# Attention's q and k as seven-product units in the first projection, with q, k and v kept in DRAM until they are used

## The chip, the cores and the metric

The kernel runs on one core of one Trainium2 chip. The metric is the device time of one execution in microseconds, from runs on the chip; a profile of one more execution shows what each engine did. TensorE (PE) multiplies into the eight banks of PSUM; VectorE (DVE), ScalarE (ACT) and GpSimd (POOL) compute; SyncE (SP) and POOL issue DMA transfers, which all run on the core's 16 DMA engines.

## The reference

One encoder layer on x of 512 x 2048, in float32:

```
h = rmsnorm(x);  proj = h @ w_in          # 2048 x 6176 columns
aq, ak, av   1024 columns each            # attention, 16 heads of 64
gq, gk 512 each, gv, gr 1024 each, glr 32 # gated linear attention (GLA), 4 heads
attn = mixture of dilated windows(aq, ak, av, relative bias)
gla  = bidirectional gated linear attention(gq, gk, gv, gates from glr), normed, gated by silu(gr)
x = x + concat(attn, gla) @ w_out
x = x + (silu(h2 @ w_gate) * (h2 @ w_up)) @ w_down      # h2 = rmsnorm(x), 5632 hidden
out = rmsnorm(x)
```

The change is in the product `proj`, and in where its results wait for attention and GLA.

## The kernel before

Every product of two float32 operands is made from halves: `hi` is the value rounded to the matmul type (made by ScalarE), `lo` the rest (made by VectorE), and hi x hi, hi x lo and lo x hi are summed in PSUM. The scale of the norm is taken out of the product: `rb[1]` (a row of 512) or `rstd1` (a column) multiplies the results.

The first projection is a list of twelve jobs, each 512 output columns over 16 k-tiles of 128 rows: `job_qk(0)`, `job_av(0)`, `job_qk(1)`, `job_qk(2)`, `job_av(1)`, `job_qk(3)`, then two pairs of gq/gk and gv, and two jobs of gr. `run_job` goes through a job in 16 halves, one k-tile each: it splits the weights three halves ahead (`Stream.split`, L198 and L199, from pieces of 512 KB that `Stream.load` fetches on SP), and issues 12 products of 512 columns (L296 to L298 in a job of kind A, whose output has the channels in the partitions; L305 to L307 in kind B, with tokens there). Four banks of PSUM gather one job.

`prep(k)` runs inside the first job: TensorE transposes one k-tile of x (L351), and `transposed` makes its hi and lo (L353, L354). `hT[k]` keeps them in SBUF for all twelve jobs. `squares1` sums the squares for the norm on ScalarE in halves 3 to 10 of the first job.

Between halves `run_side` takes steps from a list of generators, `rate` steps per half (`state["credit"]`): attention, then the low-rank gate, then GLA head by head. `run_urgent` takes one step of a second list first. One `att_step(h, b)` is a query block: two score products (L578, L579), VectorE's bias add with row minimum (L591), ScalarE's exponential (L608), reciprocal and scale on VectorE (L530, L531). For each pair of blocks two groups of four transposes (L537), copies and low halves (L603, L604), eight value products (L545, L546) and the mix of halves (L555, L557) follow in later steps. All engines execute their own instructions in the order in which the program emits them. `evac_qk` scales a job's q and k, splits them and has SP rearrange them into `QK[pr]`, one entry for each pair of heads, with SBUF to SBUF copies of 128 KB; `evac_av` fills `VS`. `gla(h)` takes 14 steps; in the last ones `L877` makes the output, `L880` its squares, `rstd_of` the scale, `L890` the scaled output, and `L896` transposes that.

The feed-forward stage already uses a seven-product scheme: `Blocks` and `Feed` compute two by two blocks of weights and activations with seven block products instead of eight. A unit is 256 columns in four pieces; `Blocks.sums` (L1159 to L1161) forms weight sums, `Blocks.split` (L1172, L1177) their halves, `Feed.products` issues 14 products of 512 columns (hi weights times hi and lo activations, L1267) and 14 of 256 (lo weights times hi, L1253) a piece, and `evac7` combines seven banks with ScalarE, VectorE and four accumulating DMA transfers of POOL. `pair_operands` makes the activation operands.

SBUF is handed out in slots: 68 of 512 columns (`s2`) and 17 of 1024 (`s4`). A transfer into a slot waits until the last user of that slot is done.

Of the kernel before, what the change touches and what calls it, by code (L numbers as in the profile page):

```python
# [117 lines left out]
def layer(nc, tc, x, attn_norm_w, w_in, rel_table, gw_f, gb_f, gw_b, gb_b, gla_norm_w, w_out,  # L118
# [7 lines left out]
    with tc.manual_schedule(), \  # L126
# [124 lines left out]
        class Job:  # L251
            drop = None
# [16 lines left out]
        def run_job(j):  # L269
# [6 lines left out]
            for i in range(j.n):  # L276
# [9 lines left out]
                for b in range(4):  # L286
                    if j.between:
                        j.between(i, b)
                    for s_, k in enumerate(ks):
# [9 lines left out]
                        else:  # L299
# [7 lines left out]
                            mm(o, xl.t[:, c], wh.t[:, w], start=False, stop=last, skip_group_check=on)  # L307
                put(wh, wl)
# [7 lines left out]
                if i < j.n - 1:  # L316
                    state["credit"] += j.rate
# [28 lines left out]

        def transposed(block, k, wc, big=False):

            b = ps.get()
            for t in range(4):  # L350
                pe.transpose(b.t[:, t * P:(t + 1) * P], block(k, t), idn)  # L351
            hi, lo = s4.pair() if big else (s2.get(F32R), s2.get(F32R))
            act.activation(hi.t, b.t, AF.Copy, scale=wcol[:, wc + k:wc + k + 1])  # L353
            dve.scalar_tensor_tensor(lo.t, b.t, wcol[:, wc + k:wc + k + 1], hi.f,  # L354
                                     op0=OP.mult, op1=OP.subtract)
            put(b)
            return hi, lo
# [45 lines left out]

        def prep(k):
            hT[k] = transposed(x_block, k, W_ATT, big=k >= KT - 3)
# [50 lines left out]
        def evac_qk(g):  # L456

            def f(banks):
                ts = []
                for i in range(4):  # L460
                    t = s2.get()
                    o = t.t
                    if i < 2:
                        o = o.rearrange("p (b c) -> p b c", c=P)[:, :, ::-1]
                        dve.tensor_tensor(o, banks[i].t.rearrange("p (b c) -> p b c", c=P),
                                          rb[1].t.rearrange("p (b c) -> p b c", c=P), op=OP.mult)
                    else:
                        dve.tensor_tensor(o, banks[i].t, rb[1].t, op=OP.mult)
                    put(banks[i])
                    ts.append(t)  # L470
                urgent.append(rest(ts))

            def rest(ts):
                yield
                for i in (0, 2, 1, 3):
                    hi, lo = s2.get(F32R), s2.get(F32R)
                    if i < 2:
                        act.activation(hi.t, ts[i].t, AF.Copy, scale=-(DH ** -0.5))
                        dve.scalar_tensor_tensor(lo.t, ts[i].t, -(DH ** -0.5), hi.f,
                                                 op0=OP.mult, op1=OP.subtract)  # L480
                    else:
                        act.copy(hi.t, ts[i].t)
                        dve.tensor_tensor(lo.t, ts[i].t, hi.f, op=OP.subtract)
                    put(ts[i])
                    pr = g * 2 + i % 2
                    e, o = s2.get(F32R), s2.get(F32R)
                    if i < 2:
                        sp.dma_start(out=e.f[0:64], in_=hi.f[0:64])
                        sp.dma_start(out=e.f[64:128], in_=lo.f[0:64])
                        sp.dma_start(out=o.f[0:64], in_=lo.f[64:128])  # L490
                        sp.dma_start(out=o.f[64:128], in_=hi.f[64:128])
                        put(hi, lo)
                        QK[pr] = [(e, o)]
                    else:
                        for src in (hi, lo):
                            if src is lo:
                                e, o = s2.get(F32R), s2.get(F32R)
                            for r in (slice(0, 64), slice(64, 128)):
                                sp.dma_start(out=e.f[r], in_=src.f[0:64])
                                sp.dma_start(out=o.f[r], in_=src.f[64:128])  # L500
                            put(src)
                            QK[pr].append((e, o))
                    yield
                if g % 2:
                    side.append(attention(g))
            return f

        def evac_av(half):
            def f(banks):
                VS[half] = []  # L510
                for t in range(4):
# [7 lines left out]
                    VS[half].append(v)  # L519
                side.append(attention(2 * half))  # L520
# [45 lines left out]
        def att_step(h, b):  # L566
# [3 lines left out]
            pair = at["pair"] if h is None or b % 2 == 0 else []  # L570
# [25 lines left out]
            if pair:  # L596
                at["pair"] = []
# [18 lines left out]
        def attention(g):  # L616
            for h in range(4 * g, 4 * g + 4):
                for b in range(4):
                    att_step(h, b)
                    yield  # L620
            if g % 2:
                att_step(None, None)
                yield
                att_step(None, None)
                yield
# [55 lines left out]

        def evac_gqk(pr):
            def f(banks):
                for i in range(4):
                    t = s2.get()
                    if i < 2:
                        dve.scalar_tensor_tensor(t.t, banks[i].t, P ** -0.5, rb[1].t,
                                                 op0=OP.mult, op1=OP.mult)
                        gq[2 * pr + i] = t
                    else:  # L690
                        dve.tensor_tensor(t.t, banks[i].t, rb[1].t, op=OP.mult)
                        gk[2 * pr + i - 2] = t
                    put(banks[i])
            return f

        def evac_gv(pr):
            def f(banks):
                gv[pr] = []
                for t in range(4):
                    if t % 2 == 0:  # L700
                        gv[pr].append(s4.get(F32, [P, 2, 512]))
                    act.activation(gv[pr][-1].t[:, t % 2], banks[t].t, AF.Copy, scale=rstd1[:, t:t + 1])
                    put(banks[t])
                for h in (2 * pr, 2 * pr + 1):
# [34 lines left out]
        def gla(h):  # L739
# [3 lines left out]

            zs = []
# [212 lines left out]
        def before0(i):  # L957
# [15 lines left out]
            if i == KT - 1:  # L973
                for c in range(4):
                    put(*xt.pop(c))

        def job_qk(g, **kw):
            seg = [(w_in, C_AQ + g * 256), (w_in, C_AK + g * 256)]
            return job("A", [piece512(seg, None, k) for k in range(0, KT, 2)], list(range(KT)), acts_h, evac_qk(g),
                       **kw)  # L980

        def job_av(half, **kw):
            job("B", [piece512(w_in, C_AV + half * 512, k) for k in range(0, KT, 2)], list(range(KT)), acts_h,
                evac_av(half), **kw)
# [8 lines left out]
        def gstart():  # L993
            side.append(low_rank())

        for pr in range(2):
# [860 lines left out]
```

## Time and profile before

| | us |
|---|---|
| three runs | 2188.8, 2189.8, 2190.48 (median 2189.8) |
| the profiled execution | 2190.33 |
| its span, first to last instruction | 2188.6 |
| TensorE busy | 2178.1 |
| VectorE busy | 1662.1 |
| ScalarE busy | 1114.4 |
| first attention step (L579) starts at | 111.8 |
| last attention step (L579) starts at | 442.9 |
| last GLA transposes (L896) start at | 675.2 |
| first wide feed-forward product (L1267) at | 905.9 |

The mean granted clock of TensorE is 0.999 of full speed. Matmuls are pipelined: the duration of one in a row of the timeline overlaps the next, so the pace is read from the starts of successive rows. A row of the timeline gives start and duration in us, engine, line, operation, out<-in with shapes, and in brackets how long the engine had been idle and what ended that. A row of windows gives the stretch, TensorE busy time and count, then weight loads, VectorE, ScalarE and GpSimd in the same way, the granted clock, the DMA engines' busy share, and GB/s.

### The profile page before, as it was taken

How to read it: one execution, taken by the hardware profiler on the slowest of the kernel's cores; microseconds unless marked ns; L12 is line 12 of the kernel's file. 1: busy time of each engine (PE TensorE's matmuls, PEld its weight loads, DVE VectorE, ACT ScalarE, POOL GpSimd, SP SyncE). 2: the span in 40 equal slices, each digit the busy share in tenths (PEclk: the TensorE clock that was granted, in tenths of full speed). 3: DMA queues.
4: the chain of work that ended last, by engine and by line, in shares of the span. 5: the costliest groups of instructions: out<-in, count | busy, mean ns of one | idle time of the engine just before them, and what ended most of it. 6: DMA issues, size and time to landing. Idle time of an engine off the chain costs nothing.

```text
span 2188.6 us, 33803 instructions
## 1 busy us (share of the span) xinstructions
PE 2178.1 (100%) x12490; PEld 1912.8 (87%) x12490; DVE 1662.1 (76%) x2889; ACT 1114.4 (51%) x2045; POOL 254.9 (12%) x338
## 2 busy tenths in 40 slices
PE   9999999999999999999999999999999999999998
PEld 7888888888888888988888888888888899999987
DVE  4356665655456656899999899898998888897895
ACT  5344454543444334555555555555555665565462
POOL 0000000000000210022111221112221220021300
PEclk9999999999999999999999999999999999999999
DMA  6525534342325892376767767777767975476982
GB/s 210 171 75 160 156 94 134 94 125 58 97 78 174 297 326 88 106 185 173 185 183 182 189 174 185 183 183 186 182 183 179 277 206 175 164 188 147 285 315 77
DMA packets 251507, 373.65 MB, mean 171 GB/s; under 512 B 18701, under 2 KB 153021, under 8 KB 251342
## 3 DMA queue, kind: packets, MB, share of 16 engines
q1 hardware_dynamic: 208478, 280.89, 40.7%
q0 software_dynamic: 42544, 90.07, 19.0%
q8 instruction: 99, 1.62, 0.3%
q14 instruction: 66, 0.54, 0.1%
q10 hardware_dynamic: 320, 0.53, 0.1%
HBM read 268.60 MB, written 51.71 MB: 146 GB/s over the span
## 4 chain that ended last, share of the span: by engine, by line
PE 93%; issue 5%; DVE 1%; DMA 0%; SPq 0%; POOL 0%; ACT 0%; DVEq 0%; POOLq 0%; ACTq 0%
PE ps L1267 24%; PE ps L1253 12%; PE ps L305 6%; PE ps L306 6%; PE ps L307 6%; PE ps L298 5%; PE ps L296 5%; PE ps L297 5%; PE ps L1564 5%; PE ps L1565 5%; PE ps L1563 5%; PE ps L537 1%; PE ps L877 1%; PE ps L546 1%; PE ps L545 1%
## 5 line engine op out<-in xcount | busy, mean ns | idle before, releaser
L1267 PE MATMUL ps<-a,b 128*128 128x512 f32 x2352 | 652.2, 393 | 0.4 <-ACT b L1172 0.2
L1172 ACT CAST b<-b 128x1024 fp32r<-128x1024 f32 (+1 forms) x473 | 432.6, 944 | 292.5 <-DVE b L1177 154.3
L1177 DVE TENSOR_TENSOR b<-b,b 128x1024 fp32r<-128x1024 f32 (+1 forms) x473 | 496.3, 1084 | 32.6 <-ACT b L1172 14.5
L1267 PEld LDWEIGHTS ps<-a,b 128*128 128x128 f32 x2352 | 394.4, 188 | 42.2 <-ACT b L1172 0.7
L1253 PEld LDWEIGHTS ps<-a,b 128*128 128x128 f32 x2352 | 373.0, 189 | 59.2 <-DVE b L1177 0.5
L1253 PE MATMUL ps<-a,b 128*128 128x256 f32 x2352 | 385.3, 280 | 0.0
L199 DVE TENSOR_TENSOR a<-b,a 128x512 fp32r<-128x512 f32 x291 | 195.6, 686 | 126.4 <-ACT a L198 122.3
L1564 PE MATMUL ps<-b,a 128*128 128x256 f32 x896 | 253.7, 283 | 0.0
L1565 PE MATMUL ps<-b,a 128*128 128x256 f32 x896 | 253.6, 283 | 0.0
L1563 PE MATMUL ps<-b,a 128*128 128x256 f32 x896 | 253.6, 283 | 0.0
L198 ACT CAST a<-b 128x512 fp32r<-128x512 f32 x291 | 171.2, 618 | 56.1 <-DMA b<-in_w_in_dram 18.4
L305 PE MATMUL ps<-a,a 128*128 128x512 f32 x464 | 182.6, 394 | 0.0
L306 PE MATMUL ps<-a,a 128*128 128x512 f32 x464 | 180.7, 390 | 0.0
L307 PE MATMUL ps<-a,a 128*128 128x512 f32 x464 | 180.7, 389 | 0.0
L1564 PEld LDWEIGHTS ps<-b,a 128*128 128x128 f32 x896 | 172.0, 192 | 0.3 <-DVE b L1177 0.2
L1563 PEld LDWEIGHTS ps<-b,a 128*128 128x128 f32 x896 | 172.0, 192 | 0.0
L1565 PEld LDWEIGHTS ps<-b,a 128*128 128x128 f32 x896 | 172.0, 192 | 0.0
L296 PE MATMUL ps<-a,a 128*128 128x512 f32 x416 | 167.5, 403 | 0.0
L298 PE MATMUL ps<-a,a 128*128 128x512 f32 x416 | 163.0, 392 | 0.1
L297 PE MATMUL ps<-a,a 128*128 128x512 f32 x416 | 162.8, 391 | 0.0
L1159 DVE TENSOR_TENSOR b<-b 128x512 f32<-128x512 f32 x212 | 145.3, 685 | 16.8 <-DMA b<-in_w_down_dram 9.7
L307 PEld LDWEIGHTS ps<-a,a 128*128 128x128 f32 x464 | 87.1, 188 | 18.4
(263 smaller groups left out, 3349.7 us busy)
## 6 DMA issues: line engine op xcount, KB each, us to landing
b<-in_w_gate_dram SPq DMA_DIRECT2D x109, 512.0 KB, 4.0
b<-in_w_up_dram SPq DMA_DIRECT2D x88, 512.0 KB, 3.9
b<-in_w_down_dram SPq DMA_DIRECT2D x88, 512.0 KB, 5.4
b<-a POOLq DMA_DIRECT2D x126, 256.0 KB, 4.5
b<-in_w_in_dram SPq DMA_DIRECT2D x48, 512.0 KB, 4.2
b<-in_w_in_dram SPq DMA_DIRECT2D x92, 256.0 KB, 4.3
b<-in_w_out_dram SPq DMA_DIRECT2D x32, 512.0 KB, 5.9
a<-a SPq DMA_DIRECT2D x96, 128.0 KB, 2.3
```

What stands on the lines that cost most here:

```text
L296: mm(o, wh.t[:, c], xh.t, start=first, stop=False)
L298: mm(o, wl.t[:, c], xh.t, start=False, stop=last)
L305: mm(o, xh.t[:, c], wh.t[:, w], start=first and not on, stop=False, skip_group_check=on)
L306: mm(o, xh.t[:, c], wl.t[:, w], start=False, stop=False, skip_group_check=on)
L307: mm(o, xl.t[:, c], wh.t[:, w], start=False, stop=last, skip_group_check=on)
L1172: act.copy(o, src)
L1177: dve.tensor_tensor(o, src, h, op=OP.subtract)
L1253: mm(o, wl, xh, start=False, stop=end, skip_group_check=True)
L1267: mm(o, wh, x_.rearrange("p s t -> p (s t)"), start=first and p == 0, stop=False, skip_group_check=True)
L1563: mm(o, xh[:, t], wh, start=first and h == 0, stop=False, skip_group_check=True)
L1564: mm(o, xh[:, t], wl, start=False, stop=False, skip_group_check=True)
L1565: mm(o, xl[:, t], wh, start=False, stop=last, skip_group_check=True)
```

## The change

The eight 256-column blocks of aq and ak leave the job list and become eight units of the feed-forward scheme (`Front`, a subclass of `Feed`). The order is now: v's two jobs, the eight units, then gq/gk, gv and gr as before. To have SBUF for the units' operands, `prep` writes hi and lo of the transposed x also to DRAM (`xhd`), `load_h` reads them back as `hT` in the last unit, and q, k, v, gq, gk and gv are stored in DRAM by POOL (`qkd`, `vd`, `gqd`, `gvd`) and read on SP when attention or GLA needs them. Attention is now one generator over all 16 heads, started with the first gq/gk job. The six remaining jobs run at 1.45 steps a half, with a quarter of that credit after each bank (`fine`). A pair of query blocks is transposed one step later than before.

```diff
+                    if j.fine and b < 3:
+                        state["credit"] += j.rate / 4
+                        if state["credit"] >= 1:
+                            state["credit"] -= 1
+                            run_side(1)
...
         def prep(k):
-            hT[k] = transposed(x_block, k, W_ATT, big=k >= KT - 3)
+            hB[k] = [s2.get(F32R, [P, 2, 256]) for _ in range(2)]
+            for n, o in enumerate(hB[k]):
+                act.activation(o.t[:, 0], b.t[:, c], AF.Copy, scale=w)
+                dve.scalar_tensor_tensor(o.t[:, 1], b.t[:, c], w, o.f[:, 0], op0=OP.mult, op1=OP.subtract)
+            fB[k] = s2.get()
+            act.activation(fB[k].t, b.t, AF.Copy, scale=w)
+            for n, o in enumerate(hB[k]):
+                pool.dma_start(out=xhd[k][:, :, n * 256:(n + 1) * 256], in_=o.f)
+            if k % 2:
+                side.append(sums_x(k // 2))
...
+        def sums_x(q):
+            sub(t13.t[:, a], f1.t[:, a], f1.t[:, z])
...
+            for n, (name, f, h) in enumerate((("T2", t24, a), ("T4", t24, z), ("T1", t13, a), ("T3", t13, z))):
+                act.copy(o.t[:, 0], f.t[:, h])
+                sub(o.t[:, 1], f.t[:, h], o.f[:, 0])
...
+        def load_h(k):
+                for n in range(2):
+                    sp.dma_start(out=hT[k][n].f, in_=xhd[k][:, n])
...
+        def load_qk(pr):
+            for i in range(2):
+                sp.dma_start(out=ts[i].t, in_=qkd[pr // 2 * 2 + i][:, f * 512:(f + 1) * 512])
+            yield
+            for i in range(2):
+                act.activation(hv, src, AF.Copy, scale=scale)
+                dve.scalar_tensor_tensor(lv, src, scale, hf, op0=OP.mult, op1=OP.subtract)
...
+        def load_v(half):
+            for t in range(4):
+                sp.dma_start(out=VS[half][t].f.rearrange("p h s c -> p (h s c)"), in_=vd[4 * half + t])
...
-            pair = at["pair"] if h is None or b % 2 == 0 else []
+            if h is None or b % 2:
+                pair, at["pair"] = at["pair"][:2], at["pair"][2:]
...
+        def attention():
+            for h in range(NH):
+                if h % 2 == 0 and h // 2 + 1 < NH // 2:
+                    urgent.append(load_qk(h // 2 + 1))
+                while h // 2 not in ready:
+                    run_urgent()
...
-        job_qk(0, rate=1.0, before=before0, start=start0, limit=3).between = between0
-        job_av(0)
-        job_qk(1, rate=0.8)
-        job_qk(2, rate=0.8)
-        job_av(1, rate=0.8)
-        job_qk(3, rate=1.0, start=gla_operands)
+        job_av(0, before=before0, start=start0, limit=3).between = between0
+        job_av(1, before=before_front).drop = drop_b
...
+        RATE = 1.45
...
+        class Front(Feed):
+            def finish(self, u, c_, c):
+                dve.tensor_tensor(c_.t, c_.t, rb[1].t[:, None, :].to_broadcast([P, 2, 512]), op=OP.mult)
+                pool.dma_start(out=qkd[u], in_=c)
+            def run(self):
+                for i, (u, q) in enumerate(self.seq):
+                    self.load()
+                    self.split(i)
+                    self.sums(i + 1)
+                    self.sums(i + 2)
+                    self.split(i + 1)
+                    self.products(i, banks[u])
+                    if u == len(self.units) - 1:
+                        for p in (2 * q, 2 * q + 1):
+                            put(*xi.pop(p)["slots"])
+                            load_h(2 * p)
+                            load_h(2 * p + 1)
+                        if q == self.per - 1:
+                            urgent.append(load_qk(0))
+                            load_v(0)
+                    if q == self.per - 1:
+                        done = self.evac7(u, banks.pop(u))
+                        next(done)
+                    run_urgent()
```

The lines of the diff above are its core; within a function, lines that only fetch or return slots are left out.

More of the change, by code (lines that the diff above doesn't have):

```diff
@@ L345, in rows_of @@
             return s
[L347 to L357, printed above, removed]
         def weighted(tiles, k, wc):
@@ L407, in squares1, with drop_b @@
+        def drop_b(k):
+            if k % 2 == 0:
+                put(hB[k][1])
+        def load_h(k):
+            if k < KT - 3:
+                hT[k] = (s2.get(F32R), s2.get(F32R))
+                for n in range(2):
+                    sp.dma_start(out=hT[k][n].f, in_=xhd[k][:, n])
+            else:
+                hT[k] = s4.pair()
+                for n in range(2):
+                    sp.dma_start(out=hT[k][n].f, in_=xhd[k][:, n])
         def squares1(c, t):
@@ L518, in f @@
                     put(banks[t])
-                    VS[half].append(v)
-                side.append(attention(2 * half))
+                    pool.dma_start(out=vd[4 * half + t], in_=v.f.rearrange("p h s c -> p (h s c)"))
+                    put(v)
             return f
@@ L972, in before0, with before_front @@
                 rb[1] = rows_of(rstd1)
[L973 to L980, printed above, removed]
-        def job_av(half, **kw):
-            job("B", [piece512(w_in, C_AV + half * 512, k) for k in range(0, KT, 2)], list(range(KT)), acts_h,
-                evac_av(half), **kw)
-        job_qk(0, rate=1.0, before=before0, start=start0, limit=3).between = between0
-        job_av(0)
-        job_qk(1, rate=0.8)
-        job_qk(2, rate=0.8)
-        job_av(1, rate=0.8)
-        job_qk(3, rate=1.0, start=gla_operands)
+            if i in (5, 7, 10, 14):
+                put(*xt.pop((5, 7, 10, 14).index(i)))
+        def job_av(half, **kw):
+            return job("B", [piece512(w_in, C_AV + half * 512, k) for k in range(0, KT, 2)], list(range(KT)), acts_b,
+                       evac_av(half), rate=1.0, **kw)
+        def before_front(i):
+            if i >= 9:
+                fr.load()
+            if i in (11, 13):
+                fr.sums(i // 2 - 5)
+            if i == 14:
+                fr.split(0)
+        job_av(0, before=before0, start=start0, limit=3).between = between0
+        job_av(1, before=before_front).drop = drop_b
+        st.until = len(st.pieces)
         def gstart():
+            side.append(attention())
             side.append(low_rank())
+        n_front = len(jobs)
+        RATE = 1.45
         for pr in range(2):
```

203 lines of the change are left out of this document (135 added, 68 removed).

## The prediction

> **What bounds the kernel now.** I read the page first, then TensorE's stretches in the chain of waits, then the timelines of VectorE and ScalarE at the places that the change touches.
>
> ```profile
> span 2188.6 us, 33803 instructions
> PE 2178.1 (100%) x12490; PEld 1912.8 (87%) x12490; DVE 1662.1 (76%) x2889; ACT 1114.4 (51%) x2045; POOL 254.9 (12%) x338
> PE 93%; issue 5%; DVE 1%; DMA 0%; SPq 0%; POOL 0%; ACT 0%; DVEq 0%; POOLq 0%; ACTq 0%
> ```
>
> TensorE is never without work: no other engine has more than 1% of the chain. So whatever shortens TensorE's instructions shortens the span in full, and whatever makes TensorE wait lengthens it in full; the kernel has no slack that could absorb either. The first projection must be judged by both.
>
> **What the seven products save.** The timeline of TensorE in the attention stage, and the chain in the feed-forward stage:
>
> ```profile
> 328.61 0.28 PE L545 MATMUL ps<-b,b 128*128 128x256 f32 x1
> ...
> 329.56 0.40 PE L296 MATMUL ps<-a,a 128*128 128x512 f32 x1
> ...
> 332.31 0.39 PE L578 MATMUL ps<-a,a 128*128 128x512 f32 x1
> ```
> ```profile
> 1009.76 3.20 PE ps L1267 x14
> 1012.96 1.67 PE ps L1253 x14
> ...
> 1029.26 3.20 PE ps L1267 x14
> ...
> 1048.76 3.20 PE ps L1267 x14
> ```
>
> Twelve products of 512 columns take 332.31 - 329.56 = 2.75 us, 0.229 each. 256 columns of q or k cost 16 x 2 x 3 = 96 of them now: 21.98 us. As a unit they are four pieces of 14 wide and 14 narrow products, 3.20 + 1.67 = 4.87 us a piece, and a unit starts every 1029.26 - 1009.76 = 19.50 us. Eight units: 8 x (21.98 - 19.50) = **-19.9 us**. Transposes, attention and GLA keep their own products.
>
> **Do the new units run at that pace?** VectorE makes sums, low halves and the combination:
>
> ```profile
> 1029.26:1068.26 39.00, 39.00 (x226) 34.24 (x225) 35.58 (x56) 21.47 (x37) 7.57 (x9) 1.00 0.72 183
> ```
> ```profile
> 1029.13 0.68 DVE L1159 TENSOR_TENSOR b<-b 128x512 f32<-128x512 f32 x1
> 1029.85 0.42 DVE L1160 TENSOR_TENSOR b<-b,b 128x256 f32<-128x256 f32 x1
> 1030.30 0.43 DVE L1161 TENSOR_TENSOR b<-b,b 128x256 f32<-128x256 f32 x1
> 1030.65 2.08 DVE L1177 TENSOR_TENSOR b<-b,b 128x768 fp32r<-128x768 f32 x2
> ```
>
> Two units there hold VectorE 35.58 of 39.00 us with seven sums of 1.52 us (1030.65 - 1029.13), one being read ready-made. The front's pairs make all eight: 37.1 of 39.0. It fits, by 5%, and I take no cost; if the combination's waits broke it, a unit would grow by up to 2 us (a rival).
>
> **v's first job.** The order of the built program shows that `prep` now issues on ScalarE two activations of 256 columns and one of 512 where it had one of 512, and each `sums_x` four casts of 256 for two k. ScalarE in this job before:
>
> ```profile
> 29.11 0.60 ACT L198 CAST a<-b 128x512 fp32r<-128x512 f32 x1
> 30.51 0.69 ACT L353 ACTIVATE a<-ps,wcol 128x512 fp32r<-128x512 f32 x1 [0.79 <-PE ps L351]
> ...
> 32.33 0.61 ACT L198 CAST a<-b 128x512 fp32r<-128x512 f32 x1
> ```
> ```profile
> L1051 ACT CAST a<-a 128x256 fp32r<-128x256 f32 x56 | 20.5, 405 | 12.4 <-DVE a L1043 11.1 <-PE ps L307 1.1
> ```
>
> A half takes 32.33 - 29.11 = 3.22 us and leaves ScalarE 0.79 free. Two more casts of 0.40 and a third of 1.6 (four per three yields) add 1.3: 0.5 too much in six halves, 1.3 in the two whose squares come in quarters, 5.5 us in all. TensorE transposes one and a half halves ahead, about 3.2 us after the operands' own latency, so 2.3 us come through: **+2.3** (0 to 5.5). The 32 writes of `xhd` on POOL's queue only have to be back before the last unit.
>
> **The first attention step.** Call T the end of the last front product. The built order puts the first head's two score products (L648, L649) after nine products of the next job, at T+2.1. What they need stands on SP in this order: 32 loads of `xhd` (256 KB), four of v (512 KB), a weight piece (512 KB), then q and k of the first pair (2 x 256 KB), their twelve rearranging copies, and then the two bias tables. Each load waits for the one eight before it, and the eighth load of `xhd` also for product 23 of 28 of the last unit's first piece: T - 19.5 + 23/28 x 4.87 = T - 15.5. Behind that stand 25 x 0.26 + 2.1 + 0.5 + 0.5 = 9.7 MB. Windows of the busiest and of a poorer stretch, and landing times:
>
> ```profile
> 775.00:780.00 5.00, 5.00 (x27) 4.22 (x27) 0.86 (x3) 1.53 (x3) 2.12 (x4) 1.00 1.07 389
> 15.00:20.00 5.00, 5.00 (x26) 4.14 (x25) 2.70 (x4) 3.95 (x11) 0.00 (x0) 1.00 0.88 283
> ```
> ```profile
> a<-a SPq DMA_DIRECT2D x96, 128.0 KB, 2.3
> b<-line SPq DMA_DIRECT2D x16, 448.0 KB, 4.6
> ```
>
> At 389 GB/s this is 25 us. The accumulating copies of the unit before run in the same time: the 39 us window has 0.72 x 39 = 28.1 us of the DMA engines' time for 183 x 39 = 7.1 MB, which would be 18.4 at 389, so a unit's accumulations hold them 4.9 us. Hence 30 us: q and k land at T+14.5, are split (0.63 and 0.69), copied (2.3), and TensorE may go on at T+18.5; the bias, issued after the copies, lets VectorE reduce the first scores at T+22 instead of T+2.6. TensorE's queue is strictly behind L648: the job's own products wait there too, and ScalarE and VectorE stand at the split of q, with the casts of later weights behind it. I take **+20** (11 with no accumulation in the way, 27 at 283 GB/s).
>
> [...]
>
> **Attention's pace.** The job before gave a step per 12 products, now 1.45: 8.3 products between steps. VectorE, before:
>
> ```profile
> 320.40 0.69 DVE L591 CUSTOM_DVE_ANT_0 a<-ps,b 128x512 f32<-128x512 f32 x1 [0.54 <-PE ps L579]
> ...
> 322.43 0.43 DVE L557 TENSOR_TENSOR a<-ps,a 64x256 f32<-64x256 f32 x1 [1.33 <-ACT a L555]
> 323.55 0.69 DVE L372 TENSOR_TENSOR a<-a,a 128x512 fp32r<-128x512 f32 x1 [0.69 <-ACT a L371]
> 324.15 0.16 DVE L530 RECIPROCAL small<-small 128x1 f32<-128x1 f32 x1
> ...
> 325.47 0.69 DVE L591 CUSTOM_DVE_ANT_0 a<-ps,b 128x512 f32<-128x512 f32 x1
> 326.08 0.08 DVE L591 DVE_READ_ACCUMULATOR2_ANT small<- 128x1 f32 x1
> 326.08 1.28 DVE L604 TENSOR_TENSOR b<-ps,b 128x512 fp32r<-128x512 f32 x2
> ...
> 327.87 0.68 DVE L199 TENSOR_TENSOR a<-b,a 128x512 fp32r<-128x512 f32 x1
> 328.81 0.69 DVE L591 CUSTOM_DVE_ANT_0 a<-ps,b 128x512 f32<-128x512 f32 x1 [0.25 <-PE ps L579]
> ...
> 330.84 0.42 DVE L557 TENSOR_TENSOR a<-ps,a 64x256 f32<-64x256 f32 x1 [1.34 <-ACT a L555]
> ...
> 331.76 0.69 DVE L199 TENSOR_TENSOR a<-b,a 128x512 fp32r<-128x512 f32 x1
> ```
>
> A step with a mix takes 331.76 - 328.81 = 2.95 us, of which 1.34 is a wait for ScalarE (exponential, then copy) that no other instruction fills; the changed order keeps it. A step with a pair takes 327.87 - 325.47 = 2.40. Eight steps (two heads): 4 x 2.95 + 4 x 2.40, the mix's own split 1.4 (324.15 - 322.43 less 0.34), 5.5 weight halves of 0.61, and two new splits of q and k of 0.62: 27.4 us. TensorE for the same: 66 products of 0.229, 16 score products, and 0.95 (329.56 - 328.61) for each of four transposed pairs and four value products: 26.4. Before, 96 products made it 33.2, and VectorE waited for TensorE; now TensorE waits, held by four free banks of ps. 60 steps: 7.5. Evacuating gq/gk once (four ops, 2.7 us) and the late second pair of q and k, whose load stands in the queue behind the last unit's combination, add to VectorE's chain: **+11** (0 where the waits overlap, 17 where all of them add).
>
> **GLA.** It also runs 1.45 times as densely.
>
> ```profile
> 503.47 4.48 PE L877 MATMUL ps<-b,a 128*128 128x256 f32 x20
> ...
> 513.28 1.03 PE L896 MATMUL ps<-idn,b 128*128 128x128 f32 x8
> ```
> ```profile
> 511.64 1.57 ACT L890 ACTIVATE b<-ps,small 128x256 f32<-128x256 f32 x4 [0.83 <-DVE small L334]
> ```
>
> The output's transposes start at 513.28, when L890 ends (513.21): no slack. Two gaps of 2.75 become 1.90, so TensorE is there 1.7 us too early; one cast less in the chain leaves about 1.1. Four heads: **+4.5** (1 to 9, the larger with a like wait at the gated q and k).
>
> **Sum.** 2188.6 - 19.9 + 2.3 + 20 + 11 + 4.5 = 2206.5 of span. The profiled execution took 2190.33 for 2188.6, the runs' median is 2189.8: 1.2 to 1.7 more. **2208 us.** All low: 2188.6 - 19.9 + 0 + 11 + 0 + 1 + 1.5 = 2182; all high: 2188.6 - 19.9 + 5.5 + 27 + 17 + 9 + 1.5 = 2229.
>
> **Rivals.**
> *Attention stays with TensorE.* Its waits overlap: only the first step is late, 17 us at TensorE instead of 20 at VectorE, and some 2 us of catching up. 2188.6 - 19.9 + 2.3 + 19 + 4.5 + 1.5 = 2196. For it: VectorE's excess is 1.0 us in 26.4. Against: its waits are measured, and nothing stands beside them.
> *The first q and k come in time*: faster. The place is T, the price 20 us, and it decides where they land before T+5: the loads of `xhd` would have to start a unit earlier or the queue to move about twice 389 GB/s; by its other waits alone SP could issue them at T-6.6. Then VectorE has the bias early too, and with attention's waits overlapped: 2188.6 - 19.9 + 2.3 + 2 + 0 + 3 + 1.5 = 2178. Against: with its DMA engines fully busy (share 1.07) the quoted window moves 389 GB/s.
> *The front is bound by VectorE.* 37.1 of 39 leaves 1 us a unit; if each unit grew by 2 us, the gain goes: 2224.
> That the change does what it says is certain by the built order: 448 wide and 448 narrow products in the front against 768 wide ones.
>
> **Chances.** Forecast 0.50, TensorE's attention 0.24, in time 0.18, front bound 0.08. The runs tell 0.2% (4.4 us) from no change. In-time gives 0.17 faster and 0.01 same; of the second case some 0.06 lie within 2194; the rest is slower: faster 0.17, same 0.07, slower 0.76. The range leaves out the in-time case and little above: 2185 to 2227.
>
> **What would show it.** Front units every 19.5 us; TensorE idle before L648, released by the copies `a<-a`, for 12 to 20 us; attention's 64 steps some 3.4 us apart with TensorE waiting for VectorE; short waits before the transposes that end each GLA head. Wrong, if that idle time is under 5 us or the step time is 3.3 with no idle TensorE.

## The result, and the profile after

The changed kernel takes 2270.6 us (median of 4 runs, 2264.7 to 2272.2) where the kernel before takes 2190.1 on the same chip: 1.0364 times as long, 95% interval 1.0344 to 1.0383. It is slower, as forecast, but by 80 us and not by 18. The profiled execution has a span of 2262.9 us, 74.3 more than before; it is the fastest of the four, 5.9 us under their median, and the stage times below are its own.

The page of the changed kernel: span, engines, and the rows of TensorE and its granted clock over 40 slices of 56.6 us.

```profile
span 2262.9 us, 34862 instructions
PE 2185.7 (97%) x12618; PEld 1911.0 (84%) x12618; DVE 1780.5 (79%) x3121; ACT 1184.0 (52%) x2181; POOL 316.8 (14%) x430
PE   8999948999999999999999999999999999999998
PEclk9999979999999999999999999999999999999999
```

Before, TensorE was busy for 2178.1 of 2188.6 us; now it is idle for 77. The holes are in slices 1, 6 and 7. Its waits by line and by what ended them (us in total, times, longest):

```profile
PE ps L648 <- DMA a<-a: 31.6, 2, 26.5
PE ps L612 <- DVE b L673: 6.6, 10, 0.8
PE ps L306 <- ACT a L424: 4.3, 4, 1.5
PE ps L900 <- DVE a L882: 4.1, 3, 2.7
PE ps L306 <- ACT a L198: 3.1, 3, 2.1
```

To see where the time went, cut both traces at the same places of the work. TensorE's timeline of the changed kernel at the cuts (start, length, line):

```profile
130.11 0.61 PE L1363 MATMUL ps<-a,b 128*128 128x512 f32 x2
...
285.87 0.39 PE L1349 MATMUL ps<-a,b 128*128 128x256 f32 x2
287.51 0.50 PE L297 MATMUL ps<-a,a 128*128 128x512 f32 x1 [1.25 <-ACT a L198]
...
316.59 0.76 PE L648 MATMUL ps<-a,a 128*128 128x512 f32 x1 [26.46 <-DMA a<-a]
...
351.23 0.77 PE L648 MATMUL ps<-a,a 128*128 128x512 f32 x1 [5.09 <-DMA a<-a]
...
559.21 0.28 PE L612 MATMUL ps<-b,b 128*128 128x256 f32 x1
...
757.34 0.39 PE L299 MATMUL ps<-b,a 128*128 128x512 f32 x1
```

and of the kernel before, at the first score, the last value product and the last product of the first projection's gates:

```profile
111.62 0.39 PE L578 MATMUL ps<-a,a 128*128 128x512 f32 x1
...
451.25 0.28 PE L546 MATMUL ps<-b,b 128*128 128x256 f32 x1
...
683.25 0.39 PE L298 MATMUL ps<-b,a 128*128 128x512 f32 x1
```

Before, TensorE never stood in these stretches, so they give the price of its work; the products are counted in the built programs. Attention's 339.8 us hold 1228 products of 512 columns at 0.2292; the rest, 58.3, is 0.114 for each of 256 transposes and 256 value products. GLA's 232 us hold some 834 (good to two products, 0.4 us), and 40.7 of its own. "Own work" below is what TensorE would need at those prices for each stage of the changed kernel; the loss is the stage less that. T is 287.51 - 1.25 = 286.3.

| stage of the changed kernel | own work | took | loss | predicted |
|---|---|---|---|---|
| v's two jobs, to 130.1 | 111.6 - 24 x 0.2292 = 106.1 | 130.1 | 24.0 | 2.3 |
| front, to T = 286.3 | 8 x 19.5 = 156.0 | 156.1 | 0.1 | 0 |
| T to the first score | 9 products: 2.1 | 30.3 | 28.2 | 20 (at VectorE) |
| first 8 steps, to 351.2 | 82 x 0.2292 + 40 x 0.114 = 23.4 | 34.6 | 11.2 | with the next |
| other 56 steps, to 559.2 | 592 x 0.2292 + 472 x 0.114 = 189.5 | 208.0 | 18.5 | 11, both |
| GLA and gates, to 757.3 | 637 x 0.2292 + 40.7 = 186.7 | 198.1 | 11.4 | 4.5 |

The own work is 663.8 us, 19.5 less than the 683.2 of before: the seven products save what was forecast. The losses are 93.4. Behind this place both kernels need the same 1505 us.

The largest miss is the first row. Timelines of ScalarE and of VectorE for one half of v's first job in the changed kernel:

```profile
47.95 0.47 ACT L424 ACTIVATE a<-ps,wcol 128x256 fp32r<-128x256 f32 x1
49.20 0.48 ACT L424 ACTIVATE a<-ps,wcol 128x256 fp32r<-128x256 f32 x1 [0.78 <-DVE a L425]
50.23 0.69 ACT L427 ACTIVATE a<-ps,wcol 128x512 f32<-128x512 f32 x1 [0.55 <-DVE a L425]
...
52.55 0.47 ACT L424 ACTIVATE a<-ps,wcol 128x256 fp32r<-128x256 f32 x1
...
57.76 0.47 ACT L424 ACTIVATE a<-ps,wcol 128x256 fp32r<-128x256 f32 x1
```
```profile
48.08 0.69 DVE L199 TENSOR_TENSOR a<-b,a 128x512 fp32r<-128x512 f32 x1 [1.29 <-ACT a L198]
48.69 0.48 DVE L425 SCALAR_TENSOR_TENSOR a<-ps,wcol,a 128x256 fp32r<-128x256 f32 x1
49.71 0.49 DVE L425 SCALAR_TENSOR_TENSOR a<-ps,wcol,a 128x256 fp32r<-128x256 f32 x1 [0.54 <-ACT a L424]
```

The three scaled copies of one bank don't run one behind the other on ScalarE. The second stands until VectorE has made the low half of the first, the third until that of the second, and the first low half itself is queued behind a weight's (L199). That is 0.78 + 0.55 = 1.33 us of standing per half; a half takes 57.76 - 52.55 = 5.2 us, and 4.6 where it holds no casts of sums, against 3.2 before. The granted clock (column before the DMA share) is lower there too: 0.95 and 0.88 in the first two stretches of 40 us, where the kernel before has 1.00 in both. So the loss of 24 us is standing and slower running together.

```profile
0.00:40.00 40.00, 33.07 (x127) 24.99 (x128) 15.90 (x35) 20.39 (x49) 9.32 (x17) 0.95 0.95 333
40.00:80.00 40.00, 34.48 (x143) 23.82 (x142) 20.76 (x51) 28.51 (x72) 11.45 (x17) 0.88 0.64 216
290.00:316.00 26.00, 0.13 (x1) 0.00 (x0) 2.56 (x3) 1.26 (x2) 0.56 (x1) 0.60 0.90 319
316.00:330.00 14.00, 11.68 (x46) 9.34 (x47) 5.16 (x14) 3.63 (x9) 1.71 (x2) 0.77 0.99 286
```

The second and third copies take nothing from a low half; what they share with it is the bank that both read, and they stand 0.78 and 0.55 us until it is made. Why the built program orders two reads of one bank isn't shown.

At the transition the mechanism is the one forecast, only longer. The loading queue of the changed kernel:

```profile
268.58 23.34 SPq L472 DMA_DIRECT2D a<-xhd  x26
292.28 3.65 SPq L476 DMA_DIRECT2D b<-xhd  x6
296.31 3.52 SPq L573 DMA_DIRECT2D b<-vd  x4
300.19 1.01 SPq L183 DMA_DIRECT2D b<-in_w_in_dram  x2
301.50 1.00 SPq L536 DMA_DIRECT2D a<-qkd  x2
```
```profile
309.38 0.63 ACT L547 ACTIVATE a<-a 128x512 fp32r<-128x512 f32 x1 [20.88 <-DMA a<-qkd]
```

q and k are issued at T + 15.2 and split from T + 23.1 on (forecast: landed at T + 14.5); TensorE goes on at T + 30.3 (forecast T + 18.5), at a granted clock of 0.77 for the next 14 us.

### The profile page after: what moved, and what is told of

Read it like the earlier page. It is cut to its first block, busy times and chain, and to the rows that moved or that the text cites. A ratio compares the mean times of both kernels' runs of the same rounds, so it can differ in the third digit from the quotient of the medians.

```text
span 2262.9 us, 34862 instructions
## 1 busy us (share of the span) xinstructions
PE 2185.7 (97%) x12618; PEld 1911.0 (84%) x12618; DVE 1780.5 (79%) x3121; ACT 1184.0 (52%) x2181; POOL 316.8 (14%) x430
## 4 chain that ended last, share of the span: by engine, by line
PE 52%; DMA 2%; DVE 2%; issue 0%; ACT 0%; POOL 0%; DVEq 0%; ACTq 0%; POOLq 0%
PE ps L1363 23%; PE ps L1349 12%; PE ps L1712 5%; PE ps L1713 5%; PE ps L1711 5%; DMA b<-a 1%; PE ps L306 1%; PE ps L308 1%; PE ps L307 1%; PE ps L1905 0%; PE ps L1903 0%; PE ps L1904 0%; DMA xd<-a 0%; DVE b L1272 0%; DMA gd<-b 0%
## 5 line engine op out<-in xcount | busy, mean ns | idle before, releaser
L1363 PE MATMUL ps<-a,b 128*128 128x512 f32 x2800 | 776.3, 393 | 0.4 <-ACT b L1267 0.2
L1267 ACT CAST b<-b 128x768 fp32r<-128x768 f32 (+1 forms) x537 | 490.6, 945 | 322.0 <-DVE b L1272 159.3
L1272 DVE TENSOR_TENSOR b<-b,b 128x768 fp32r<-128x768 f32 (+1 forms) x537 | 563.1, 1084 | 33.7 <-ACT b L1267 14.5
L1363 PEld LDWEIGHTS ps<-a,b 128*128 128x128 f32 x2800 | 469.6, 188 | 50.1 <-ACT b L1267 0.7
L1349 PEld LDWEIGHTS ps<-a,b 128*128 128x128 f32 x2800 | 444.0, 189 | 70.4 <-DVE b L1272 0.5
L1349 PE MATMUL ps<-a,b 128*128 128x256 f32 x2800 | 458.7, 280 | 0.1
L199 DVE TENSOR_TENSOR a<-b,a 128x512 fp32r<-128x512 f32 x227 | 153.7, 686 | 86.7 <-ACT a L198 82.5
L306 PE MATMUL ps<-a,a 128*128 128x512 f32 x488 | 197.3, 404 | 7.4 <-ACT a L424 4.3
L307 PE MATMUL ps<-a,a 128*128 128x512 f32 x488 | 193.9, 397 | 1.3 <-DVE a L199 1.3
L308 PE MATMUL ps<-a,a 128*128 128x512 f32 x488 | 193.6, 397 | 0.0
L1254 DVE TENSOR_TENSOR b<-b 128x512 f32<-128x512 f32 x244 | 167.1, 685 | 16.9 <-PE ps L1712 7.3
L198 ACT CAST a<-b 128x512 fp32r<-128x512 f32 x227 | 134.7, 618 | 38.5 <-DMA b<-in_w_out_dram 15.0
L306 PEld LDWEIGHTS ps<-a,a 128*128 128x128 f32 x488 | 93.1, 191 | 30.4 <-ACT a L424 6.3
L307 PEld LDWEIGHTS ps<-a,a 128*128 128x128 f32 x488 | 93.2, 191 | 21.5 <-DVE a L199 3.9
L308 PEld LDWEIGHTS ps<-a,a 128*128 128x128 f32 x488 | 93.0, 191 | 21.1 <-DVE a L425 1.5
L1256 DVE TENSOR_TENSOR b<-b,b 128x256 f32<-128x256 f32 x244 | 103.8, 425 | 8.4
```

The lines of the kernel that those rows point to most:

```text
L199: dve.tensor_tensor(h[3].t, r, h[2].f, op=OP.subtract)
L306: mm(o, xh.t[:, c], wh.t[:, w], start=first and not on, stop=False, skip_group_check=on)
L307: mm(o, xh.t[:, c], wl.t[:, w], start=False, stop=False, skip_group_check=on)
L1254: dve.tensor_tensor(s_[:, :, 0:2], r[:, :, 1:3], r[:, :, 0:1].to_broadcast(shape), op=OP.add)
L1267: act.copy(o, src)
L1272: dve.tensor_tensor(o, src, h, op=OP.subtract)
```

## Experiments

All run beside the kernel before, whose median was 2189.2 to 2189.4 us in each set; "less" or "more" is against the changed kernel's 2270.6 where nothing else is said. Stage times are cut as above, each from one profiled execution. The diffs give the edits in shortened form. "Transition" is the loss from the front's start to the ninth step, 39.5 us in the changed kernel (0.1 + 28.2 + 11.2).

**1. The order in `prep`.**

```diff
-    for each half n: act -> hi(n); dve -> lo(n)
-    act -> full copy
+    act -> hi(0); act -> hi(1); act -> full copy
+    dve -> lo(0); dve -> lo(1)
```

> Each x block's three scaled copies on ScalarE are issued one behind the other, and both low halves on VectorE behind them; nothing else moves. Theory (v's first job lost 24 us because ScalarE and VectorE take turns at one bank of ps, 0.78 + 0.55 us of ScalarE waiting per half): the half goes from 5.2 to about 3.9 us, TensorE's idle time before L306 in the first 110 us is nearly gone and the whole falls by 14 to 20 us, to 2251 to 2257. Rival one (ScalarE is simply overloaded by the three extra casts): the waits move, the half stays at 5.0 us or more, the whole falls by under 5 us. Rival two (the 32 writes of xhd and the loads of x and of the weights share the DMA engines): no change, 2266 to 2274.

2251.2 us (ratio to before 1.0276, 1.0259 to 1.0293): 19.4 less. v's two jobs take 113.2 us, 16.9 less, and all other stages are within 2 us of the changed kernel's. ScalarE in that kernel:

```profile
42.07 0.86 ACT L424 ACTIVATE a<-ps,wcol 128x256 fp32r<-128x256 f32 x2
42.79 0.72 ACT L426 ACTIVATE a<-ps,wcol 128x512 f32<-128x512 f32 x1
...
45.71 0.88 ACT L424 ACTIVATE a<-ps,wcol 128x256 fp32r<-128x256 f32 x2
```

A half takes 3.64 us with the same instructions. VectorE's row shows the turns at the bank once more: the low halves now wait for the full copy (L426), which reads the same bank and makes nothing that they use.

```profile
40.50 0.88 DVE L428 SCALAR_TENSOR_TENSOR a<-ps,wcol,a 128x256 fp32r<-128x256 f32 x2 [0.63 <-ACT a L426]
```

So it was the turn-taking at the bank, and not the load (rival one) or the writes (rival two), which this order keeps. In the eight kernels with the old order v's two jobs take 129.0 to 131.1 us; in e1, e4, e8 and e10, where only the order is changed in that stage, 111.6 to 113.2. The saving holds the clock too: over v's two jobs it averages 0.95 in the changed kernel and 0.98 in e1. 7 us remain in that stage.

**2. Who holds up the first scores.**

```diff
+    unit 6, last piece:  load q, k of pair 0
+    unit 7, pieces 0, 1: split and copy them; load two bias tables
     unit 7: load xhd 0..15, then v
-    after unit 7: load q, k of pair 0
```

> The loads of the first pair of q and k are issued before the last unit of the front, their splits and copies and the two bias tables in its first two pieces, ahead of the 32 loads of xhd. Theory (the first step stands for 30 us behind 9.7 MB on the loading queue): TensorE has no wait of over 3 us before the first L648, and the whole falls by 22 to 32 us, to 2239 to 2249; the second pair may still be 5 us late. Rival (the DMA engines are full and whatever comes last is late): the wait moves to the first value products or to the job's own products, which wait for v or for xhd, and the whole falls by under 12 us.

2267.6: 3.0 less. The rival holds. The first score comes 8.9 us behind the front, but the next steps take 57.3 and not 34.6. ScalarE, whose queue VectorE follows, stood for weights that now came behind xhd and v:

```profile
321.18 0.62 ACT L198 CAST a<-b 128x512 fp32r<-128x512 f32 x1 [18.98 <-DMA b<-in_w_in_dram]
```

> The order of e1_prep_order and the early first pair of e2_first_pair_early together. If the two losses are independent the savings add: 36 to 52 us less than 2270.6, that is 2219 to 2235, still slower than before by 29 to 45. If the second hides part of the first (a front that starts earlier has the same queue to wait for), less than the sum.

2251.1, as experiment 1 alone: the early pair adds nothing to it.

Next, xhd in the order of use, with the second pair and the weights between:

```diff
     unit 7: load xhd 0..7, then v
+    next job, half i: load xhd i + 8; at i = 1, 3, 4: load, split q, split k of pair 1
```

> As e2_first_pair_early, and the 32 loads of xhd are issued in the order of their use: 8 k blocks in the last unit of the front, the other 8 one per half of the next job, so that weight pieces and the second pair of q and k stand between them. Theory (the 30 us are a queue in the wrong order, since the transfers needed at T are few): the 8.7 us and the 15.9 us that e2 showed both go, as does the wait for the second pair; stage from the front's end to the ninth step 66 to about 32 us; the whole 30 to 40 us less than the changed kernel, 2231 to 2241. Rival (the DMA engines have no room at all here, with the accumulating copies): the wait is at some other load, the whole falls by under 15 us, 2256 or more.

2248.9: 21.7 less, between the two theories. Transition 25.5. ScalarE's longest wait there:

```profile
ACT a L1402 <- DMA a<-a: 14.5, 1, 14.5
```

The wait went to a third place, the front's last evacuation, which writes over a tile that the copies of q and k still read. So the pair goes a unit earlier:

```diff
-    unit 6, last piece; unit 7, pieces 0, 1: load, split q, split k of pair 0
+    unit 6, pieces 0, 1, 2: the same
```

> As e5_due_order, but the first pair of q and k is loaded, split and copied in the unit before the last, so that its copies are through the queue before the first load of xhd. In e5 TensorE stood 14.9 us at the job's first weights: the front's last evacuation wrote over a tile that those copies still read, and the copies shared full DMA engines with the loads of xhd. Theory (the transfers are few enough, only their order was wrong): no wait of over 3 us between the front's end and the ninth step; that stretch, 64.9 us in the changed kernel and 50.8 in e5, is 28 to 34; the whole 12 to 19 us less than e5, 2230 to 2237. Rival (bandwidth: the DMA engines are full until all that the last unit issues has landed): a wait of 8 us or more stays at some other transfer, 2241 or more.

2250.0, no gain over e5. That wait is gone; now 5.9 us stand inside the front and 7.2 at L297. On the loading queue the weight pieces come behind the copies, which themselves wait for VectorE's split; that this makes the 5.9 us is read from the order of the queue, and no run shows it. Transition 22.5.

Half of the loads of xhd, at the changed kernel's own order (what the kernel computes is then another result; only its time is of use):

```diff
     def load_h(k):
+        if k >= 8: hT[k] = hT[k - 8]
```

> The changed kernel with half of the loads of xhd left out: the k blocks 8 to 15 are computed with the operands of 0 to 7, so 16 loads (4.2 MB) and not 32 stand ahead of v and of the first q and k. Theory (the wait before L648 is the bytes ahead in the queue, moved at the 274 to 312 GB/s of that stretch): the wait of 26.5 us falls by 4.2 MB / 0.29 = 14 us to 11 to 14, the whole by 12 to 16, 2255 to 2259. Rival (the wait is the queue's own order of semaphores, the last unit's combination or the splits): it falls by under 6 us, 2264 or more.

2254.3: 16.2 less. TensorE's waits between 284 and 342 us:

```profile
PE ps L650 <- DMA a<-a: 20.2, 2, 15.1
```

The longest falls from 26.5 to 15.1: 11.4 us for 4.2 MB, 368 GB/s, where 14 us were forecast. So much of its length goes with the loads ahead of q and k. The run leaves out transfers as well as bytes, so it doesn't tell these apart, and what makes up the 15.1 us that are left isn't shown.

**3. Attention and GLA.**

```diff
-    RATE = 1.45 in all six jobs
+    1.3 in the first three, 1.6 in the last three
```

> The side steps run at 1.3 for the first three jobs behind the front (attention) and at 1.6 for the last three (GLA) in place of 1.45 throughout; their number is the same. Theory (from the third pair of q and k on, attention loses some 14 us because VectorE's chain is longer than TensorE's work per step, GLA 12 us because its steps are too close): attention's waits for L673 and L661 go, 8 to 12 us saved there, GLA loses 3 to 6 more; 2260 to 2268. Rival (the losses of the attention stage all come from late loads of q and k): attention's waits stay, GLA loses 3 to 6, 2272 to 2277.

> 1.6 for the first three jobs (attention), 1.3 for the last three (GLA). e3 with 1.3 and 1.6 lost 2.2 us more in attention and 6 more in GLA. If GLA's loss goes by density, it falls from 11.4 to 5 to 7 us. Theory (attention's loss is a burst per pair): its excess over TensorE's own work stays at 18 to 22, the whole 2263 to 2268. Rival (VectorE bound on the mean: steps stay 3.6 us apart while TensorE needs only 3.2): the excess goes to 35 or more and the whole to 2280.

e3 took 2268.4, e7 2273.2. Losses of the last 56 attention steps: 20.7 at 1.3, 18.5 at 1.45, 26.1 at 1.6; of GLA and gates: 10.1 at 1.3, 11.4 at 1.45, 17.3 at 1.6. Neither theory's numbers fit: more distance doesn't free attention, less costs some.

```diff
-    h even, ahead of step 0: queue the loads and splits of the next pair
+    h even, ahead of step 2: the same
```

> Only the place of the loads and splits of the next pair of q and k in the attention changes: behind the third step of a pair and not ahead of its first. Theory (each pair's 2 us of waits at L611 and L612 are a burst: the two splits of q and k fall in the same steps as the split of the last mix, and TensorE's free banks hold it off for about a step only): the waits at L611 and L612 fall from 9 to under 5 us, the stage from the ninth step on from 208 to 201 to 204, the whole by 3 to 7 us, to 2264 to 2268. Rival (VectorE's chain is longer than TensorE's on the mean over all eight steps, so that the place does not matter): 208 stays, 2270 to 2273.

2267.4, a number that the theory would give, but the stage took 209.9 against 208.0: no gain where it should be, and the 3 us of the whole are within the spread of the changed kernel's runs. The waits at L611 and L612 do fall, from 8.3 to 5.3 us, but those at L648 for ScalarE and VectorE grow from 1.0 to 3.5, and the granted clock is 0.97 for 0.99. So the burst theory's gain doesn't come. The waits on TensorE's timeline in the changed kernel:

```profile
396.43 0.39 PE L649 MATMUL ps<-a,a 128*128 128x512 f32 x1
397.31 0.36 PE L611 MATMUL ps<-b,b 128*128 128x256 f32 x1 [0.49 <-DVE small L661]
398.42 0.39 PE L612 MATMUL ps<-b,b 128*128 128x256 f32 x1 [0.75 <-DVE b L673]
```

The value products stand for the low halves that VectorE makes behind its own wait of 1.33 us for the mix copy (that wait is 38.3 us in all in this stage). A later run, e12, puts work into it, and one more step into each GLA head. It builds on e11, which moves the sums of x in e10; e10 is e9 with the order of e1.

> e9_pair_a_unit_earlier with the order of e1_prep_order: 17 to 20 us less than e9 if the two are independent, 2211 to 2219. What is left over before is then v's first job 7, attention 18 and GLA 11 to 13 us, less the front's 20.

2233.5: 16.5 less than e9, a little under the sum.

```diff
-    job_av(0), job_av(1): rate = 1.0, 1.0
+    job_av(0), job_av(1): rate = 0.25, 1.6
```

> e10 with the sums of x and their casts (L439 to L450) moved from v's first job to its second: side steps at 0.25 and 1.6 in place of 1.0 and 1.0. Theory (the 7 us that e1 left in v's first job are ScalarE's load by those casts): v's two jobs take 107 to 109 us in place of 113, the whole 4 to 6 less than e10. Rival (the loads of x and of weights set the pace of that job, its DMA engines are 90% busy in the first 40 us): 112 or more, no change.

2236.8, 3.3 more than e10. v's jobs go from 111.6 to 109.3, less than forecast, and the stages behind lose more: the transition 24.4 against 22.3, GLA and gates 14.4 against 13.1.

```diff
+    after the score's reduce, in steps with a mix:
+        dve -> low half of the next q, of the next k, or of the last mix
     mix copy on ScalarE, then VectorE's add
+    gla(h): one more step ahead of the products of gated q and k
```

> e11, and in attention the low halves of the next q and k and of the last mix run in VectorE's wait of 1.33 us for the mix copy (ScalarE's part stays one step earlier), and in each GLA head one more step stands before the products of the gated q and k. Theory (attention's 18 us are VectorE's chain: it is as long as TensorE's work and 5.3 us of every eight steps in it are that wait): filling it saves about 2 us per eight steps, the stage from the ninth step on falls from 208 to 195 to 200, GLA's waits at L900 (4 us) go; the whole 10 to 15 less than e11, about 2195. Rival (the waits are ScalarE's: exponential, copy, casts one behind the other): attention stays at 205 or more.

2214.3 (ratio to before 1.0114, 1.0099 to 1.0129): 22.5 less than e11. The last 56 steps fall from 212.6 to 200.9 us, their loss from 23.8 to 12.1; GLA and gates from 203.2 to 193.9, their loss to 5.1. Its waits in the attention stage:

```profile
PE ps L712 <- DMA a<-a: 5.3, 1, 5.3
PE ps L667 <- DVE b L739: 4.2, 7, 2.3
```

VectorE's wait for the mix copy falls from 37.2 to 25.1 us in this stage, TensorE's waits at the value products from 11.8 to 4.7. So work in that wait takes away half of e11's loss in attention; against the changed kernel's 18.5 the loss is 6.4 less. The moved low halves also stand at other places in VectorE's queue, which this run doesn't separate.

> e12 with the side steps at 1.55 in place of 1.45 and nothing else: what the density alone costs. Theory (attention is bound by VectorE's chain of about 27 us per eight steps, GLA by its own chain): attention's excess over TensorE's own work rises from 12 by 5 to 10 us, GLA's from 5 by 1 to 4; the whole 2218 to 2228. Rival (there is slack in both since the low halves fill the gap): within 3 us of e12, 2211 to 2217.

2229.3. Attention's loss is 13.3, 1.2 more: there the slack of the rival. GLA's is 17.3, 12 more, which no theory had; the waits shown in that stage are 8.8 us in all, so the rest isn't explained.

**4. Together, and what is left of the transition.**

> The order of e1, the loads of e5 and the later splits of e6 in one kernel. If the three are independent: 19 + 30 to 40 + 3 to 7 less than 2270.6, that is 2204 to 2219; still above before (2189) by the 7 us that v's first job keeps, GLA's 11 and the rest of attention's waits, less the front's 20.

2229.8: e1's order, e5's loads and e6's later splits are 40.8 less, about e1's and e5's savings added; 2204 to 2219 was missed since e5 had saved less than forecast and e6 next to nothing. Transition 22.1.

```diff
-    unit 7: load xhd 0..7;  next job, half i: load xhd i + 8
+    unit 7: load xhd 0..5;  next job, half i: load xhd i + 6
+    copies of pair 0 one piece behind its splits; pair 1 in unit 7, pieces 1 to 3
```

> e12 with the transition's transfers spread: the copies of the first pair are issued a piece after their splits (the loading queue doesn't wait for VectorE), the second pair is handled in the last unit too, and only 6 of 16 k blocks of xhd are loaded in the last unit, the other 10 one per half of the next job. From the front's start to the ninth step e12 takes 203.4 us against 156 + 3 + 24 of TensorE's own work, 20 too many; the changed kernel 221. Theory A (order alone: the queue holds what is needed next behind what isn't): 186 to 192, the whole 2195 to 2204. Theory B (the DMA engines are the limit: xhd's 8.4 MB and the accumulating copies fill them whatever the order): 198 or more, the whole 2208 or more.

2216.0, 1.7 more than e12. The first score comes 3.5 us behind the front, and then TensorE waits at the first value products:

```profile
PE ps L669 <- DVE small L728: 13.6, 1, 13.6
```

The engine named there follows a chain: VectorE stood 13.1 us at L199 for ScalarE, and ScalarE 14.3 us for a weight piece, which now comes behind the copies of the second pair on the loading queue. Transition 27.1, and by its numbers theory B.

```diff
+    side.append(11 empty steps)
     side.append(attention())
+    next job: load pair 0 at half 1, bias at 2, v at 3, pair 1 at 5
```

> e12 with attention begun 11 side steps (81 products, 18.6 us) later, so that the next job works with its own weights and xhd while the first two pairs of q and k, the bias and v come, in the order of their use; side steps at 1.55 in place of 1.45, so that as many fit. Theory (the wait at the transition is due to the first use of q and k at T+2, not to the engines' or the queues' total work): from the front's start to the ninth step no wait of over 3 us; 156 + 20.6 + 22 to 26 = 199 to 203 for 81 products more, that is 20 us less lost than in e12; the whole 2195 to 2203 if the denser steps cost nothing, up to 2208 if e16 shows a cost. Rival (full DMA engines also delay the job's own weights and xhd): 8 us or more of waits at L297, 2208 or more.

2223.5. The front runs undisturbed (156.2), but the next job waits for its own weights' low halves (8.5 us at L299), and behind that, from 302.4 to 307 us, the products of 512 columns start 0.43 us apart where they start 0.23 apart before and after; transition 23.5. The rival holds.

Six kernels with four orders of the loads (e5 and e8; e9 and e12; e13; e15) leave 22 to 27 of the 39.5 us. That the loads ahead count is shown by e14; whether some order hides them all stays open. No version tried beats the kernel before.

## Why the prediction was right in sign and wrong in size

- *What the seven products save*: right. -19.9 forecast, -19.5 by the own work; the front takes 156.1 us, 19.5 a unit, with VectorE busy for 141.3 of 156.2 us (148 forecast) and no loss. The front-bound rival falls.
- *v's first job*: **this step failed**, 24.0 for 2.3 us (bounds 0 to 5.5). It added the durations of the new instructions and compared the sum with ScalarE's free time, as if they could run one behind the other. But `prep` issues activation, low half, activation, low half, activation on one bank, and the built program makes each engine wait for the other (ScalarE 0.78 and 0.55 us a half). The waits stood in the built order and cost 16.9 us, with the lower clock that came with them (0.95 over the two jobs, 0.98 in e1). The 7 us left by e1 are above the upper bound too; e11 and e12, with the casts moved, lose 3.2 and 1.9.
- *The first attention step*: right in mechanism, short in size: 28.2 us at TensorE for 20 at VectorE, above the upper bound of 27. The term took the best 5 us window of another stage (389 GB/s); the trace moved 319 GB/s while TensorE stood. The granted clock of 0.77 in the 14 us behind the stop has no term in the sum.
- *Attention's pace*: 29.7 for 11 (upper bound 17). 11.2 of it are the first eight steps. They end with 5.1 us for the copies of the second pair, and 1.4 more follow behind them; the prediction named that pair and priced it only as part of VectorE's chain. In the other steps the chain was rightly named: with work in its wait for ScalarE the loss is 12.1 in e12, against 23.8 in e11 and 18.5 here.
- *GLA*: 11.4 for 4.5 (upper bound 9), and more at another place than at the one priced: L900, the gated q and k, which the prediction named for its upper bound, waited 4.1 us, the transposes that end a head (L986) only 1.5. The waits shown in this stage are 7.2 us in all, so 4.2 of the loss stay unexplained.
- The signs named beforehand: units every 19.5 us, as seen; a stop before L648 released by `a<-a`, 26.5 us where 12 to 20 were named; steps 3.6 us apart from the ninth on, where 3.4 were named.

All four losses came out too small, by 21.7, 8.2, 18.7 and 6.9 us, and none too large to balance them. Each was built from durations and rates of the kernel before, where TensorE never stood, with little allowance for engines and queues that wait for each other, and none in the sum for the clock.

## What to carry to other kernels

Before adding instructions that read one PSUM bank on two engines, look at the order in which they are issued: all of one engine's first, then the other's. Here that alone was worth 17 us of 24. Data parked in DRAM came back in a burst at the stage where it is used; price such a burst at the rate of a stretch with like traffic (319 GB/s here), not at the best one (389), with all that must come before the first use, and remember that reordering the queue here moved the wait to the next thing that was behind (15.9 us in e2, 14.9 in e5, 13.6 in e13). Where a chain of two engines has a fixed wait in every step, put other work into it before changing its pace: 1.33 us a step with a mix here, and attention's loss fell from 23.8 us to 12.1 with work in it (e12).

## What the runs showed of the hardware

The clock granted to TensorE fell in v's first job, where its waits are short. Its longest wait there in the changed kernel, and the same 40 us of e1, which has fewer waits:

```profile
PE ps L515 <- ACT a L427: 2.8, 1, 2.8
```
```profile
40.00:80.00 40.00, 38.96 (x182) 30.35 (x181) 31.66 (x76) 31.60 (x77) 13.88 (x21) 1.00 0.84 311
```

No wait there is longer than 2.8 us and most are under 1.5; the clock granted between 40 and 80 us averages 0.88, against 1.00 in e1. Stretches of 2 us in the changed kernel show it at half speed behind a wait of 1.47 us (36.57 to 38.04) and behind the one of 2.8 us (57.98 to 60.78):

```profile
36.00:38.00 2.00, 0.57 (x3) 0.13 (x1) 0.35 (x1) 1.96 (x8) 0.00 (x0) 1.00 1.07 413
40.00:42.00 2.00, 2.00 (x8) 1.70 (x7) 0.76 (x2) 2.00 (x6) 0.69 (x1) 0.50 1.05 403
58.00:60.00 2.00, 0.00 (x0) 0.00 (x0) 1.46 (x3) 0.71 (x2) 0.69 (x1) 0.90 0.01 4
62.00:64.00 2.00, 2.00 (x4) 1.16 (x4) 0.90 (x2) 1.45 (x4) 0.00 (x0) 0.50 0.14 49
```

What sets the granted clock isn't shown. The stop of 26.5 us before L648 has 0.60 over 290 to 316 us and 0.77 in the 14 us behind it.
